# Third part of the weighted one-hot tiles: half of the groups from ScalarE to one VectorE operation, and the gathered dots placed anew

## The chip, the cores and the metric

The kernel runs on one core of a Trainium2 chip. The metric is the device time of one execution in microseconds. TensorE (PE) does matmuls, VectorE (DVE), ScalarE (ACT) and GpSimd (POOL) the rest; SyncE (SP), ScalarE and GpSimd issue DMAs.

## The reference, cut to what matters

A decoder block for 512 tokens of 1024 features: RMSNorm with adaLN, two mixers side by side (windowed attention and gated linear attention), then a retrieval layer over 16384 experts, all in float32. The change is in the last one:

```python
best_v, best_pos = lax.top_k(cand, PEER_TOPK)         # 16 experts for each of 8 heads and token
expert = jnp.take_along_axis(cand_i, best_pos, axis=-1)   # expert = 128 * i1 + i2
gates = jax.nn.softmax(best_v, axis=-1)
...
ub = jnp.take(u, eb, axis=0)                          # 128 experts of each token
hid = jax.nn.gelu(jnp.einsum('tkd,td->tk', ub, xb), approximate=False) * gb
vb = jnp.take(v, eb, axis=0)
return jnp.einsum('tk,tkd->td', hid, vb)
```

## The kernel before

**Tiling.** The tokens are four blocks of 128. Blocks 0, 1 and 2 (DENSE) are done densely: hidden values of all 16384 experts by matmuls, weighted with a gate matrix that is zero for experts a token does not use, then a matmul with v. Block 3 (GB) is done by gathering its rows of u and v (`gu`, `gv`). The last 64 tokens of block 2 (SB) are mixed: their hidden values come from gathered rows of u, while their v side is dense. So the dense u side has 320 tokens (TU).

**The u side.** `u_part(c)` does 128 experts: SP loads `u` (two parts to 1 MB), ScalarE writes the rounded half `his` (L71), VectorE the rest `los` (L72), TensorE does 24 matmuls of 128x320 (L78 to L80) into `ph`, ScalarE the gelu into `ge` (L967), and its queue writes pairs to DRAM (`gsp`, L984).

**The gate matrix.** For each token, `gate_group` makes the 128x128 matrix of its gates as a product of two one-hot matrices, one with a row for the first key and one, weighted by the gate, for the second. Each step, a unit here, takes 8 tokens (TB); a q is 16 tokens, two units (t0 = 0 and 8), and 48 units make the three blocks. A gate in float32 is split into three bf16 parts so that bf16 matmuls add up to it. A unit is

- `one_hot`: one VectorE operation of 128x2048 that writes `o12`, both one-hot tiles, written one unit ahead (L1185);
- `o2`: one VectorE operation that weights the second one-hot tile with parts one and two (`gp3`) (L1204);
- `o3`: eight ScalarE activations of 128x128 that weight it with part three, the float32 remainder `gr3` read as a per-partition scale (L1208);
- 24 matmuls of 128x128 into `pg`, three to a token (L1215), and two ScalarE evictions into `gs` (L1217).

Every second q `gs` is written to `Gd` in DRAM. The parts come from `gate_turn` (L1163, L1164), `gate_parts` (L1170, L1171) and `gate_rest` (L1177).

**The gathered dots.** There are 64 rows of 128 experts. `sp_gather(m)` has POOL issue an indirect DMA of 128 rows of u, 512 KB, into `spr` (L1290), a ring of three; `sp_dot(m)` multiplies and sums on VectorE (L1296) and then issues the gather of row m + 3 into the freed place.

**Order.** VectorE and POOL run in the order in which the code is written; for ScalarE, TensorE and SP a scheduler sets the order. The code is written by generators: `work` chains the head (routing of the blocks, with dots between pieces in `between`, each piece followed by `breath()`, a tiny VectorE operation) and `woven`, once for each block, which takes the four yields of a q (two for each unit) and puts a dot behind each but the first, so three a q. Each piece yields its nominal cost on VectorE and TensorE, and the loop at the end issues a `u_part` whenever TensorE's share lags:

```python
for dd, pp in work:
    d, p = d + dd, p + pp
    while u_ahead.n < NL_U and p * DVE_ALL < (d + LEAD_U) * PE_ALL:
        ...
        d, p = d + 1.14, p + UCOST
```

After this stage the remaining u parts and all v matmuls follow, into six accumulators.

Of the kernel before, what the change touches and what calls it, by code (L numbers as in the profile page):

```python
# [17 lines left out]
P = 128  # L18
D = 1024
# [30 lines left out]
def peer_block_kernel(ctx: ExitStack, tc: tile.TileContext, a: dict, out: bass.AP):  # L50
    nc = tc.nc
# [140 lines left out]
    for L in LW:  # L192
        m = 64 >> L
# [947 lines left out]
    trs = {}  # L1141


    TB = 8

    pair = lambda v: v.rearrange("p (g r) -> p g r", r=2)

    def gate_transposes(n, t1=P):

        t12 = rt.tile([P, P // 2, 2, 2], BF, tag="t12", bufs=2, name=f"t12{n}")  # L1150
        for s in range(2):
            pt = bank(f"tr{s}{n}", BK[s])
            tr = nc.tensor.transpose(pt[:, :P], I12[n][:, s], ident)
            nc.scalar.activation(t12[:, :, s], pair(pt[:, :P]), AF.Copy)
        gp3 = rt.tile([P, P // 2, 2, 2], BF, tag="gp3", bufs=2, name=f"gp3{n}")
        r = rt.tile([P, P], F32, tag="gr3", bufs=2, name=f"gr3{n}")
        trs[n] = [t12, gp3, r, None]
        gate_transposes.tr = gate_transposes.tr or tr
        yield from gate_turn(n, 0, t1)

    def gate_turn(n, t0, t1):
        pt = bank(f"trg{n}{t0}", BK[2])
        nc.tensor.transpose(pt[:, t0:t1], gates[n][t0:t1], ident[t0:t1, t0:t1])  # L1163
        nc.scalar.activation(trs[n][1][:, t0 // 2:t1 // 2, 0], pair(pt[:, t0:t1]), AF.Copy)  # L1164
        trs[n][3] = pt
        yield 0, 0.5

    def gate_parts(n, t0=0, t1=P):
        gp3, r, pt = (pair(t[:, t0:t1]) if len(t.shape) == 2 else t[:, t0 // 2:t1 // 2] for t in trs[n][1:])
        nc.vector.tensor_tensor(r, pt, gp3[:, :, 0], OP.subtract)  # L1170
        nc.scalar.activation(gp3[:, :, 1], r, AF.Copy)  # L1171
        trs[n][3] = None
        yield 0.25, 0

    def gate_rest(n, t0=0, t1=P):
        gp3, r = trs[n][1][:, t0 // 2:t1 // 2], pair(trs[n][2][:, t0:t1])
        nc.vector.tensor_tensor(r, r, gp3[:, :, 1], OP.subtract)  # L1177
# [11 lines left out]
        return o12  # L1189

    def gate_group(bi, n, q):
        gp3, low = trs[n][1:3]
        H = TB // 2
        if q % 2 == 0:
            gate_group.gs = rt.tile([P, P // CG, 2, CG, TG], F32, tag="gs", bufs=2, name=f"gs{n}{q}")
        gs = gate_group.gs
        for t0 in range(0, TG, TB):
            g0 = (q * TG + t0) // 2
            o12 = gate_group.next or one_hot(n, g0)
            gate_group.next = one_hot(n, g0 + H) if g0 + H < P // 2 else None  # L1200
            yield 1.14, 0
            o2 = rt.tile([P, H, 2, P, 2], BF, tag="o2", bufs=3, name=f"o2_{n}{q}{t0}")
            o3 = rt.tile([P, TB, P], BF, tag="o3", bufs=3, name=f"o3_{n}{q}{t0}")
            nc.vector.tensor_tensor(o2, o12[:, :, 1, None].to_broadcast([P, H, 2, P, 2]),  # L1204
                                    gp3[:, g0:g0 + H, :, None].to_broadcast([P, H, 2, P, 2]), OP.mult)
            for i in range(TB):
                g, r = divmod(i, 2)
                nc.scalar.activation(o3[:, i], o12[:, g, 1, :, r], AF.Copy,  # L1208
                                     scale=low[:, 2 * g0 + i:2 * g0 + i + 1])
            for f in range(TB // 4):  # L1210
                pt = bank(f"pg{n}{q}{t0}{f}", BK[f]).rearrange("p (a b) -> p a b", a=4)
                for i in range(4):
                    g, r = divmod(4 * f + i, 2)
                    for m in range(3):
                        nc.tensor.matmul(pt[:, i, :], o12[:, g, 0, :, r], o2[:, g, m, :, r] if m < 2 else o3[:, 4 * f + i],  # L1215
                                         start=(m == 0), stop=(m == 2))
                evict = nc.scalar.activation(gs[:, :, q % 2, :, t0 + 4 * f:t0 + 4 * f + 4],  # L1217
                                             pt.rearrange("p a (c i) -> p c i a", c=P // CG), AF.Copy)
            evicts.append(evict)
            yield 1.14, 1.4  # L1220
        k = bi * (P // TG) + q
        if bi == len(DENSE) - 1:
            nc.scalar.activation(gates_r[0][:, k], gs[:, 0, q % 2], AF.Copy)
        if q % 2:
            writes.append(lambda: (nc.gpsimd if k >= NGRP - 3 else nc.sync).dma_start(
                Gd[:, :, k - 1:k + 1].rearrange("c p g e -> p c (g e)"), gs.rearrange("p c g i t -> p c (g i t)")))
            if k != NGRP - 3:
                writes.pop()()
# [32 lines left out]
    def sp_index(i):  # L1261
        c0, n = SETS[i]
        s0 = c0 - (TD - P)
        if i == 0:
            sp["e"] = rt.tile([P, P], I32, name="spe")
            nc.vector.scalar_tensor_tensor(sp["e"], I12[SB][:, 0], 128.0, I12[SB][:, 1], op0=OP.mult, op1=OP.add)
        sp["ix", i] = rt.tile([P, n], I32, name=f"spix{i}")
        sp["g", i] = rt.tile([P, n], F32, name=f"spg{i}")
        sp["hid", i] = rt.tile([P, n], F32, name=f"sphid{i}")
        for src, key, dt in ((sp["e"], "ix", I32), (gates[SB], "g", F32)):  # L1270
            if i == 0:
                for r in range(P // n):
                    nc.sync.dma_start(sp[key, i][r * n:(r + 1) * n], src[s0:s0 + n, r * n:(r + 1) * n])
            else:
                d = dr.tile([P // n, n, n], dt, name=f"d{key}{i}")
                nc.sync.dma_start(d.rearrange("r t j -> t r j"), src[s0:s0 + n].rearrange("t (r j) -> t r j", j=n))
                nc.sync.dma_start(sp[key, i], d.rearrange("r t j -> (r t) j"))
        if i == 0:
            for j in range(3):
                sp_gather(j)  # L1280
        yield 0.3, 0

# [2 lines left out]
    def sp_gather(m):  # L1285
        i, j = sp_all[m]
        if m == 0:
            sp["r"] = gk.tile([P, 3, D], F32, tag="gring", bufs=1, name="spr")
        sp[m] = sp["r"][:, m % 3]
        nc.gpsimd.indirect_dma_start(out=sp[m], out_offset=None, in_=a["u"],  # L1290
                                     in_offset=bass.IndirectOffsetOnAxis(ap=sp["ix", i][:, j:j + 1], axis=0))

    def sp_dot(m):
        i, j = sp_all[m]
        r = sp.pop(m)
        nc.vector.scalar_tensor_tensor(r, r, 1.0, sp["x", i], op0=OP.mult, op1=OP.mult,  # L1296
                                       accum_out=sp["hid", i][:, j:j + 1])
        if m + 3 < TS:
            sp_gather(m + 3)
        elif m == TS - 1:  # L1300
            sp.pop("r")
        yield 1.15, 0

    def sp_finish(i):
        c0, n = SETS[i]
# [159 lines left out]
    def woven(n, rows, extra, rests={}):  # L1465
        for q in range(P // TG):
            for i, piece in enumerate(gate_group(DENSE.index(n), n, q)):
                yield piece
                if i == 0 and q in rests:
                    yield from rests[q]  # L1470
                if i and rows:
                    yield from sp_dot(rows.pop(0))
                if n == SB and i % 2 and q >= places[0][1]:
                    breath()
                    yield 0.15, 0
            if q in extra:
                yield from chain(*extra[q])
            if writes:
                writes.pop()()

    def breath():
        nc.vector.scalar_tensor_tensor(junk[:, :2], ident[:, :2], 1.0, ident[:, :2], op0=OP.mult, op1=OP.mult,
# [14 lines left out]
    second_block = {1: [route(GB)], 2: [gathered_index()], 6: [gate_transposes(SB, P // 2)], 7: [gate_parts(SB, 0, P // 2)]}
    second_block[7].append(first_place())
# [381 lines left out]
```

## Time and profile before

| | us |
|---|---|
| runs of the kernel before | 1467.71, 1467.70, 1465.24; median 1467.7 |
| profiled execution | 1466.82 |
| its span, first to last instruction | 1465.0, granted clock 0.995 |
| head of the change's stage: routing to the first one-hot tile | 446.1 to 504.9 |
| first two blocks of gates | 504.9 to 702.9 |
| third block of gates | 702.9 to 767.4 |
| its last matmuls | to 776.6 |

A row of a group of instructions names line, engine, operation and tiles, then busy time and mean length in ns, then the idle time before them and what ended it. A row of waits names who waited for whom: microseconds in total, times, and the longest. A timeline row gives start and length in us, and in brackets the idle time before it. A row of windows gives the stretch, its length, the busy time of each engine with the count of its instructions, the granted clock, the busy share of the DMA engines and GB/s.

### The profile page before, as it was taken

Reading aid. Unit: us, or ns where it says so; the run is one execution under the profiler, and the core shown is the slowest. Engines: PE = TensorE matmul, PEld = TensorE weight load, DVE = VectorE, ACT = ScalarE, POOL = GpSimd, SP = SyncE. Lnnn points to the kernel's source line nnn. Section 1 sums busy time; section 2 is a strip of 40 time slices with the busy share of each in tenths; the row PEclk is TensorE's granted clock in tenths of the full one; section 3 lists DMA queues with packets and bytes.
Section 4 is the critical chain, followed back from the end, with each engine's and each line's share of the span. In section 5 each row is a group of like instructions: output and inputs, shape, how many; then the busy total and the mean of one; then the engine's idle time right before and its main releaser. Section 6 shows DMA issues by size and latency. Waiting matters only on the chain. (4 is left out here: it accounts for less than half of the span.)

```text
span 1465.0 us, 23919 instructions
## 1 busy us (share of the span) xinstructions
PE 1408.5 (96%) x9020; PEld 1250.4 (85%) x9020; DVE 1261.0 (86%) x2308; ACT 716.0 (49%) x1299; POOL 603.1 (41%) x401
## 2 busy tenths in 40 slices
PE   5999899999999899999989999999999999999997
PEld 4788788888899899999978888888888888888885
DVE  7777867589999798999976899999999999889996
ACT  4556476533344498878895333233333333232333
POOL 2000000044523344424024676776677676555520
PEclk9999999999999999999999999999999999999999
DMA  9622636354257899999779999999999999999962
GB/s 358 235 87 84 206 113 204 123 189 155 99 195 279 280 319 348 361 347 364 288 254 396 412 412 410 413 412 413 409 410 398 405 372 412 400 411 411 411 252 72
DMA packets 129972, 443.82 MB, mean 303 GB/s; under 512 B 11953, under 2 KB 48577, under 8 KB 109505
## 3 DMA queue, kind: packets, MB, share of 16 engines
q1 hardware_dynamic: 71120, 256.39, 46.3%
q0 software_dynamic: 47136, 171.99, 30.5%
q10 hardware_dynamic: 11600, 13.93, 2.7%
q8 instruction: 70, 1.15, 0.3%
q14 instruction: 46, 0.37, 0.1%
HBM read 399.70 MB, written 42.47 MB: 302 GB/s over the span
## 5 line engine op out<-in xcount | busy, mean ns | idle before, releaser
L78 PE MATMUL ph<-h2Th,his 128*128 128x320 f32 x1024 | 321.5, 314 | 11.0 <-ACT ge L967 9.0
L80 PE MATMUL ph<-h2Th,los 128*128 128x320 f32 x1024 | 317.0, 311 | 2.0 <-DVE los L1654 1.8
L79 PE MATMUL ph<-h2Tl,his 128*128 128x320 f32 x1024 | 316.9, 310 | 0.0
L1342 POOL DMA_INDIRECT gu<-in_u_dram,ix_u x128 | 212.2, 1657 | 149.3 <-DVE gu L1352 80.2
L1377 POOL DMA_INDIRECT gv<-in_vP_dram,ix_v x128 | 206.5, 1613 | 115.5 <-DVE gacc L1382 90.1
L78 PEld LDWEIGHTS ph<-h2Th,his 128*128 128x128 f32 x1024 | 193.6, 189 | 14.1 <-ACT ge L967 11.0
L80 PEld LDWEIGHTS ph<-h2Th,los 128*128 128x128 f32 x1024 | 193.3, 189 | 2.8 <-DVE los L1654 2.0
L79 PEld LDWEIGHTS ph<-h2Tl,his 128*128 128x128 f32 x1024 | 193.8, 189 | 0.8
L1290 POOL DMA_INDIRECT spr<-in_u_dram,spix x64 | 104.9, 1640 | 186.2 <-DVE spr L1296 141.6
L1382 DVE SCALAR_TENSOR_TENSOR gacc<-gv,hg,gacc 128x1024 f32<-128x1024 f32 x127 | 162.6, 1280 | 7.9 <-DMA gv<-in_vP_dram,ix_v 7.6
L78 PE MATMUL acc<-his,Ah 128*128 128x512 f32 x432 | 168.0, 389 | 0.0
L79 PE MATMUL acc<-los,Ah 128*128 128x512 f32 x432 | 168.0, 389 | 0.0
L80 PE MATMUL acc<-his,Al 128*128 128x512 f32 x432 | 168.0, 389 | 0.0
L1352 DVE SCALAR_TENSOR_TENSOR gu<-gu,h2n 128x1024 f32<-128x1024 f32 x128 | 155.7, 1220 | 6.7 <-DMA gu<-in_u_dram,ix_u 6.7
L78 PE MATMUL acc<-hi,Ah 128*128 128x512 f32 x336 | 131.3, 391 | 0.0
L80 PE MATMUL acc<-hi,Al 128*128 128x512 f32 x336 | 131.1, 390 | 0.0
L79 PE MATMUL acc<-lo,Ah 128*128 128x512 f32 x336 | 130.7, 389 | 0.0
L1650 ACT ACTIVATE Ah<-gr 128x768 fp32r<-128x768 f32 x64 | 53.6, 838 | 151.7 <-PE acc L79 128.5
L1208 ACT ACTIVATE o<-o,gr 128x128 bf16<-128x128 bf16 x384 | 121.6, 416 | 7.8 <-DVE o L1185 7.8
L71 ACT ACTIVATE his<-u 128x1024 fp32r<-128x1024 f32 x86 | 90.8, 1057 | 23.4 <-PE ph L79 9.5
L72 DVE TENSOR_TENSOR los<-u,his 128x1024 fp32r<-128x1024 f32 x75 | 91.2, 1218 | 9.7 <-ACT his L71 9.7
L1296 DVE SCALAR_TENSOR_TENSOR spr<-spr,xs 128x1024 f32<-128x1024 f32 x64 | 77.9, 1219 | 23.7 <-DMA spr<-in_u_dram,spix 23.7
(617 smaller groups left out, 2988.0 us busy)
## 6 DMA issues: line engine op xcount, KB each, us to landing
u<-in_uT_dram SPq DMA_DIRECT2D x43, 1024.0 KB
gr<-Gd SPq DMA_DIRECT2D x15, 1536.0 KB
Gd<-gs SPq DMA_DIRECT2D x10, 2048.0 KB
gsp<-ge ACTq DMA_DIRECT2D x40, 320.0 KB
wa<-in_w_ada_dram SPq DMA_DIRECT2D x12, 1024.0 KB
wo<-in_w_out_dram SPq DMA_DIRECT2D x8, 1024.0 KB
wq<-in_wq_dram SPq DMA_DIRECT2D x8, 1024.0 KB
wi<-in_w_in_dram SPq DMA_DIRECT2D x7, 1024.0 KB
```

The costliest lines, as they stand in the source:

```text
L71: nc.scalar.activation(hi, src, AF.Copy)
L72: lo_eng.tensor_tensor(lo, src, hi, OP.subtract)
L78: nc.tensor.matmul(acc, lh, rh, start=start, stop=False)
L79: nc.tensor.matmul(acc, lh, rl, start=False, stop=False)
L80: return nc.tensor.matmul(acc, ll, rh, start=False, stop=stop)
L1208: nc.scalar.activation(o3[:, i], o12[:, g, 1, :, r], AF.Copy, scale=low[:, 2 * g0 + i:2 * g0 + i + 1])
L1290: nc.gpsimd.indirect_dma_start(out=sp[m], out_offset=None, in_=a["u"], in_offset=bass.IndirectOffsetOnAxis(ap=sp["ix", i][:, j:j + 1], axi ...
L1296: nc.vector.scalar_tensor_tensor(r, r, 1.0, sp["x", i], op0=OP.mult, op1=OP.mult, accum_out=sp["hid", i][:, j:j + 1])
L1342: nc.gpsimd.indirect_dma_start(out=ur, out_offset=None, in_=a["u"], in_offset=bass.IndirectOffsetOnAxis(ap=ix_u[:, s:s + 1], axis=0))
L1352: nc.vector.scalar_tensor_tensor(ur, ur, 1.0, h2n, op0=OP.mult, op1=OP.mult, accum_out=hid[:, s:s + 1])
L1377: nc.gpsimd.indirect_dma_start(out=vr, out_offset=None, in_=a["vP"], in_offset=bass.IndirectOffsetOnAxis(ap=ix_v[:, s:s + 1], axis=0))
L1382: nc.vector.scalar_tensor_tensor(gacc, vr, hg[:, s:s + 1], gacc, op0=OP.mult, op1=OP.add)
```

## The change

- For the second unit of each q (t0 = 8, 24 of 48) the third part is made by one VectorE operation of 128x1024 bf16 out of a bf16 copy of the remainder, `gp1`. `gate_rest` writes `gp1` with one more ScalarE activation. For the first unit the eight activations stay.
- `o2` and `o3` become one tile `o2` of three parts, with the same bytes.
- The ring of rows is seven deep until dot 20 (HEAD): three places as before and four in a tile `spr2`, which borrows a buffer of `gs`; it is three deep from then on.
- The head holds 20 dots in place of 13, and two more breaths. The other 44 are spread singly, 44 over 51 places, by a counter in `woven`.
- The planner's nominal VectorE sum has 5.16 for each q in place of 4.56, and a unit with t0 = 8 yields 1.74 in place of 1.14.

```diff
+        gp1 = rt.tile([P, P // 2, 2], BF, tag="gp1", bufs=2, name=f"gp1{n}")
...
     def gate_rest(n, t0=0, t1=P):
...
         nc.vector.tensor_tensor(r, r, gp3[:, :, 1], OP.subtract)
+        nc.scalar.activation(trs[n][3][:, t0 // 2:t1 // 2], r, AF.Copy)
...
-            o2 = rt.tile([P, H, 2, P, 2], BF, tag="o2", bufs=3, name=f"o2_{n}{q}{t0}")
-            o3 = rt.tile([P, TB, P], BF, tag="o3", bufs=3, name=f"o3_{n}{q}{t0}")
+            o2 = rt.tile([P, H, 3, P, 2], BF, tag="o2", bufs=3, name=f"o2_{n}{q}{t0}")
...
-            for i in range(TB):
-                g, r = divmod(i, 2)
-                nc.scalar.activation(o3[:, i], o12[:, g, 1, :, r], AF.Copy,
-                                     scale=low[:, 2 * g0 + i:2 * g0 + i + 1])
+            if t0:
+                nc.vector.tensor_tensor(o2[:, :, 2], o12[:, :, 1], gp1[:, g0:g0 + H, None].to_broadcast([P, H, P, 2]),
+                                        OP.mult)
+            else:
+                for i in range(TB):
+                    g, r = divmod(i, 2)
+                    nc.scalar.activation(o2[:, g, 2, :, r], o12[:, g, 1, :, r], AF.Copy,
+                                         scale=low[:, 2 * g0 + i:2 * g0 + i + 1])
...
-            yield 1.14, 1.4
+            yield (1.74 if t0 else 1.14), 1.4
...
-            for j in range(3):
+            for j in range(7):
                 sp_gather(j)
...
-        sp[m] = sp["r"][:, m % 3]
+            sp["r2"] = rt.tile([P, 4, D], F32, tag="gs", bufs=2, name="spr2")
+        k = m % 7 if m < HEAD else m % 3
+        sp[m] = sp["r"][:, k] if k < 3 else sp["r2"][:, k - 3]
...
-        if m + 3 < TS:
-            sp_gather(m + 3)
-        elif m == TS - 1:
+        while sp_dot.next < min(TS, m + 8 if sp_dot.next < HEAD else m + 4):
+            sp_gather(sp_dot.next)
+            sp_dot.next += 1
+        if m == TS - 1:
...
                 if i and rows:
-                    yield from sp_dot(rows.pop(0))
+                    woven.place += 1
+                    if TS - len(rows) < HEAD + woven.place * (TS - HEAD) / 51:
+                        yield from sp_dot(rows.pop(0))
...
-    head = (route(SB), sp_index(0), sp_rows(0), between(route(0), (0, 0, 0)), gate_transposes(0), between(route(1), (3, 3, 3)),
-            between(gate_parts(0), (2,)), between(gate_rest(0), (2,)))
+    head = (route(SB), sp_index(0), sp_rows(0), between(route(0), (0, 0, 1)), gate_transposes(0), between(route(1), (3, 3, 3)),
+            between(gate_parts(0), (3,)), between(gate_rest(0), (3,)), between(iter([(0, 0)] * 2), (2, 2)))
...
-    DVE_ALL = 11 + 4 * 7.6 + 3 + 1.15 * TS + 2.28 * 2 * NGRP + 1.15 * EARLY + 1.14 * (NL_U - WQ_U)
+    DVE_ALL = 11 + 4 * 7.6 + 3 + 1.15 * TS + 5.16 * NGRP + 1.15 * EARLY + 1.14 * (NL_U - WQ_U)
```

What moves, at three places. VectorE at the first units, in the kernel before (the number after `o12_` is block and token pair, after `o2_` block, q and t0; `los<-u84` is the rest half of a u part):

```order
L1296 SCALAR_TENSOR_TENSOR spr_4610,sphid0_4605<-spr_4610,xs0_4645 128x1024
L1185 TENSOR_TENSOR o12_00_5129<-iot_3212,t120_4767 128x2048
L1185 TENSOR_TENSOR o12_04_5131<-iot_3212,t120_4767 128x2048
L72 TENSOR_TENSOR los_2207<-u80_5095,his_2206 128x1024
L1204 TENSOR_TENSOR o2_000_5162<-o12_00_5129,gp30_4774 128x2048
L1296 SCALAR_TENSOR_TENSOR spr_4610,sphid0_4605<-spr_4610,xs0_4645 128x1024
L1185 TENSOR_TENSOR o12_08_5203<-iot_3212,t120_4767 128x2048
L72 TENSOR_TENSOR los_2207<-u84_5205,his_2206 128x1024
L1296 SCALAR_TENSOR_TENSOR spr_4610,sphid0_4605<-spr_4610,xs0_4645 128x1024
L1204 TENSOR_TENSOR o2_008_5238<-o12_04_5131,gp30_4774 128x2048
```

The same place of VectorE in the change:

```order
L1305 SCALAR_TENSOR_TENSOR spr2_4611,sphid0_4605<-spr2_4611,xs0_4621 128x1024
L1187 TENSOR_TENSOR o12_00_5208<-iot_3212,t120_4774 128x2048
L1187 TENSOR_TENSOR o12_04_5210<-iot_3212,t120_4774 128x2048
L72 TENSOR_TENSOR los_2207<-u84_5174,his_2206 128x1024
L1205 TENSOR_TENSOR o2_000_5241<-o12_00_5208,gp30_4781 128x4x512
L1305 SCALAR_TENSOR_TENSOR spr_4610,sphid0_4605<-spr_4610,xs0_4621 128x1024
L1187 TENSOR_TENSOR o12_08_5281<-iot_3212,t120_4774 128x2048
L72 TENSOR_TENSOR los_2207<-u85_5283,his_2206 128x1024
L1305 SCALAR_TENSOR_TENSOR spr_4610,sphid0_4605<-spr_4610,xs0_4621 128x1024
L1205 TENSOR_TENSOR o2_008_5316<-o12_04_5210,gp30_4781 128x4x512
L1208 TENSOR_TENSOR o2_008_5316<-o12_04_5210,gp10_4782 128x4x256
```

The row order is the same, with the new operation at the end of every second unit; the u parts are two further on (u84 for u80), which stand ahead of the first one-hot tile now.

ScalarE at the first units, in the kernel before:

```order
L967 ACTIVATE ge72_4959<-ph74_4991 128x320
L71 ACTIVATE his_2206<-u80_5095 128x1024
L984 DMA gsp_2208<-ge72_4959 128x2x320
L967 ACTIVATE ge76_5024<-ph76_5027 128x320
L71 ACTIVATE his_2206<-u84_5205 128x1024
L1208 ACTIVATE o3_000_5163<-o12_00_5129,gr30_4775 128x128 x8
L967 ACTIVATE ge76_5024<-ph78_5062 128x320
L71 ACTIVATE his_2206<-u84_5205 128x1024
L1208 ACTIVATE o3_008_5239<-o12_04_5131,gr30_4775 128x128 x8
```

ScalarE there in the change:

```order
L967 ACTIVATE ge76_5039<-ph78_5074 128x320
L71 ACTIVATE his_2206<-u84_5174 128x1024
L1165 ACTIVATE gp31_5803<-trg10_5806 128x64x2
L984 DMA gsp_2208<-ge76_5039 128x2x320
L967 ACTIVATE ge80_5108<-ph80_5111 128x320
L967 ACTIVATE ge80_5108<-ph82_5142 128x320
L984 DMA gsp_2208<-ge80_5108 128x2x320
L71 ACTIVATE his_2206<-u85_5283 128x1024 x2
L1213 ACTIVATE o2_000_5241<-o12_00_5208,gr30_4783 128x128 x8
L967 ACTIVATE ge84_5176<-ph84_5179 128x320
```

Before, the second gelu of ge76 stands behind the first eight activations of the third part; in the change two gelus more (ge80) and both halves of u85 stand ahead of them.

ScalarE near the end of the third block, in the kernel before:

```order
L1217 ACTIVATE gs24_8339<-pg2400_8382 128x16x8x4
L1208 ACTIVATE o3_248_8413<-o12_236_8340,gr32_7682 128x128
L1208 ACTIVATE o3_250_8455<-o12_240_8410,gr32_7682 128x128 x2
L1217 ACTIVATE gs24_8339<-pg2401_8396 128x16x8x4
L1208 ACTIVATE o3_250_8455<-o12_240_8410,gr32_7682 128x128 x4
L1217 ACTIVATE gs24_8339<-pg2480_8423 128x16x8x4
L1223 ACTIVATE gr0_7835<-gs22_8135 128x128
L1208 ACTIVATE o3_250_8455<-o12_240_8410,gr32_7682 128x128 x2
L1208 ACTIVATE o3_258_8528<-o12_244_8452,gr32_7682 128x128 x8
```

The same place in the change:

```order
L71 ACTIVATE his_2206<-u8_8571 128x1024
L1213 ACTIVATE o2_250_8275<-o12_240_8211,gr32_7557 128x128 x7
L1222 ACTIVATE gs24_8168<-pg2400_8183 128x16x8x4
L1213 ACTIVATE o2_250_8275<-o12_240_8211,gr32_7557 128x128
L1222 ACTIVATE gs24_8168<-pg2401_8197 128x16x8x4
L967 ACTIVATE ge0_8135<-ph2_8215 128x320
L71 ACTIVATE his_2206<-u8_8571 128x1024
L1222 ACTIVATE gs24_8168<-pg2480_8244 128x16x8x4
L1222 ACTIVATE gs24_8168<-pg2481_8258 128x16x8x4
```

The evictions of a unit with t0 = 8 (pg2480, pg2481) now follow one another with no third-part activations between; those of o3_248 and o3_258 are gone.

More of the change, by code (lines that the diff above doesn't have):

```diff
@@ L1155, in gate_transposes @@
         gp3 = rt.tile([P, P // 2, 2, 2], BF, tag="gp3", bufs=2, name=f"gp3{n}")
+        gp1 = rt.tile([P, P // 2, 2], BF, tag="gp1", bufs=2, name=f"gp1{n}")
         r = rt.tile([P, P], F32, tag="gr3", bufs=2, name=f"gr3{n}")
-        trs[n] = [t12, gp3, r, None]
+        trs[n] = [t12, gp3, r, gp1, None]
         gate_transposes.tr = gate_transposes.tr or tr
@@ L1164, in gate_turn @@
         nc.scalar.activation(trs[n][1][:, t0 // 2:t1 // 2, 0], pair(pt[:, t0:t1]), AF.Copy)
-        trs[n][3] = pt
+        trs[n][4] = pt
         yield 0, 0.5
     def gate_parts(n, t0=0, t1=P):
-        gp3, r, pt = (pair(t[:, t0:t1]) if len(t.shape) == 2 else t[:, t0 // 2:t1 // 2] for t in trs[n][1:])
+        gp3, r, pt = trs[n][1][:, t0 // 2:t1 // 2], pair(trs[n][2][:, t0:t1]), pair(trs[n][4][:, t0:t1])
         nc.vector.tensor_tensor(r, pt, gp3[:, :, 0], OP.subtract)
         nc.scalar.activation(gp3[:, :, 1], r, AF.Copy)
-        trs[n][3] = None
+        trs[n][4] = None
         yield 0.25, 0
@@ L1191, in gate_group @@
     def gate_group(bi, n, q):
-        gp3, low = trs[n][1:3]
+        gp3, low, gp1 = trs[n][1:4]
         H = TB // 2
@@ L1201, in gate_group @@
             yield 1.14, 0
-            o2 = rt.tile([P, H, 2, P, 2], BF, tag="o2", bufs=3, name=f"o2_{n}{q}{t0}")
-            o3 = rt.tile([P, TB, P], BF, tag="o3", bufs=3, name=f"o3_{n}{q}{t0}")
-            nc.vector.tensor_tensor(o2, o12[:, :, 1, None].to_broadcast([P, H, 2, P, 2]),
+            o2 = rt.tile([P, H, 3, P, 2], BF, tag="o2", bufs=3, name=f"o2_{n}{q}{t0}")
+            nc.vector.tensor_tensor(o2[:, :, :2], o12[:, :, 1, None].to_broadcast([P, H, 2, P, 2]),
                                     gp3[:, g0:g0 + H, :, None].to_broadcast([P, H, 2, P, 2]), OP.mult)
-            for i in range(TB):
-                g, r = divmod(i, 2)
-                nc.scalar.activation(o3[:, i], o12[:, g, 1, :, r], AF.Copy,
-                                     scale=low[:, 2 * g0 + i:2 * g0 + i + 1])
+            if t0:
[6 more added lines that the diff above has]
+                                         scale=low[:, 2 * g0 + i:2 * g0 + i + 1])
             for f in range(TB // 4):
@@ L1214, in gate_group @@
                     for m in range(3):
-                        nc.tensor.matmul(pt[:, i, :], o12[:, g, 0, :, r], o2[:, g, m, :, r] if m < 2 else o3[:, 4 * f + i],
+                        nc.tensor.matmul(pt[:, i, :], o12[:, g, 0, :, r], o2[:, g, m, :, r],
                                          start=(m == 0), stop=(m == 2))
@@ L1288, in sp_gather @@
             sp["r"] = gk.tile([P, 3, D], F32, tag="gring", bufs=1, name="spr")
-        sp[m] = sp["r"][:, m % 3]
+            sp["r2"] = rt.tile([P, 4, D], F32, tag="gs", bufs=2, name="spr2")
+        k = m % 7 if m < HEAD else m % 3
+        sp[m] = sp["r"][:, k] if k < 3 else sp["r2"][:, k - 3]
+        if m == HEAD:
+            sp.pop("r2")
         nc.gpsimd.indirect_dma_start(out=sp[m], out_offset=None, in_=a["u"],
@@ L1297, in sp_dot @@
                                        accum_out=sp["hid", i][:, j:j + 1])
-        if m + 3 < TS:
-            sp_gather(m + 3)
-        elif m == TS - 1:
+        while sp_dot.next < min(TS, m + 8 if sp_dot.next < HEAD else m + 4):
+            sp_gather(sp_dot.next)
+            sp_dot.next += 1
+        if m == TS - 1:
             sp.pop("r")
         yield 1.15, 0
+    HEAD = 20
+    sp_dot.next = 7
     def sp_finish(i):
@@ L1479, in woven @@
                 writes.pop()()
+    woven.place = 0
     def breath():
```

## The prediction

> **What bounds the kernel now.** The profiled execution took 1466.8 us, 0.9 below the median of 1467.7; its span is 1465.0 us, and the sum below goes against its own times. First the busy times on the page, then the stretches around the change: routing and the head up to the first one-hot tile at 504.9 us, the first two blocks of gate building to 702.9, the third block to 767.4, its last matmuls to 776.6, and the rest.
>
> ```profile
> PE 1408.5 (96%) x9020; PEld 1250.4 (85%) x9020; DVE 1261.0 (86%) x2308; ACT 716.0 (49%) x1299; POOL 603.1 (41%) x401
> ```
>
> ```profile
> core 0: us, PE busy (x) PEld busy (x) DVE busy (x) ACT busy (x) POOL busy (x), PEclk, DMA share, GB/s
> 446.10:504.90 58.80, 58.05 (x399) 57.77 (x398) 47.96 (x84) 22.57 (x36) 23.06 (x15) 1.00 0.87 310
> 504.90:702.90 198.00, 188.75 (x1702) 184.21 (x1703) 184.92 (x226) 162.69 (x407) 80.06 (x48) 0.98 0.95 343
> 702.90:767.40 64.50, 58.83 (x602) 55.01 (x600) 52.77 (x68) 61.20 (x177) 8.75 (x6) 1.00 0.74 253
> 767.40:776.60 9.20, 9.11 (x82) 8.54 (x80) 2.31 (x4) 6.29 (x18) 2.96 (x3) 1.00 1.01 346
> 777.00:1465.00 688.00, 674.76 (x3328) 583.38 (x3328) 616.14 (x661) 240.31 (x238) 410.93 (x251) 0.99 0.95 381
> ```
>
> TensorE bounds the whole. Behind 777 it is busy 674.8 of 688 us, so an earlier end of the stage carries through to the end of the program. Inside the stage it idles 0.75 + 9.25 + 5.67 + 0.09 = 15.8 us, and VectorE has hardly more room: 10.8, 13.1 and 11.7 us idle in the first three stretches. The two pace each other here; ScalarE joins them in the third block with 61.2 of 64.5 us. What ended the idle times, in the head, in the first two blocks and in the third:
>
> ```profile
> DVE spr L1296 <- DMA spr<-in_u_dram,spix: 10.8, 4, 4.8
> ```
>
> ```profile
> DVE spr L1296 <- DMA spr<-in_u_dram,spix: 17.7, 13, 4.8
> PE ph L78 <- ACT ge L967: 8.2, 5, 4.9
> ACT o L1208 <- DVE o L1185: 7.8, 1, 7.8
> ACT his L71 <- DMA u<-in_uT_dram: 6.1, 4, 3.2
> ```
>
> ```profile
> DVE o L1185 <- PE pg L1215: 5.2, 3, 4.1
> PE pg L1215 <- ACT gs L1217: 3.2, 5, 1.8
> DVE gr L1170 <- ACT gp L1164: 3.0, 1, 3.0
> DVE gr L1177 <- ACT gp L1171: 2.6, 1, 2.6
> ```
>
> (The 4.8 us wait lies across the cut and counts in the first two answers; the 17.7 are 12.9 without it.) So VectorE waits for gathered rows, and in the third block for ScalarE and for a TensorE that waits for ScalarE. The timeline shows how the worst one reaches TensorE:
>
> ```profile
> 503.80 1.23 DVE L1296 SCALAR_TENSOR_TENSOR spr<-spr,xs 128x1024 f32<-128x1024 f32 x1 [4.80 <-DMA spr<-in_u_dram,spix]
> 504.95 2.36 DVE L1185 TENSOR_TENSOR o<-iot,t 128x2048 bf16<-128x2048 bf16 x2
> 507.23 1.22 DVE L72 TENSOR_TENSOR los<-u,his 128x1024 fp32r<-128x1024 f32 x1
> 508.36 1.22 DVE L1204 TENSOR_TENSOR o<-o,gp 128x2048 bf16<-128x2048 bf16 x1
> 506.21 2.44 ACT L1208 ACTIVATE o<-o,gr 128x128 bf16<-128x128 bf16 x8 [7.78 <-DVE o L1185]
> 503.59 0.31 PE L79 MATMUL ph<-h2Tl,his 128*128 128x320 f32 x1
> 503.73 0.31 PE L80 MATMUL ph<-h2Th,los 128*128 128x320 f32 x1
> 503.88 0.27 PE L1163 MATMUL trg<-ident,g 128*128 128x128 f32 x1
> 509.03 0.64 PE L78 MATMUL ph<-h2Th,his 128*128 128x320 f32 x1 [4.87 <-ACT ge L967]
> 509.46 0.47 PE L79 MATMUL ph<-h2Tl,his 128*128 128x320 f32 x1
> 509.73 0.47 PE L80 MATMUL ph<-h2Th,los 128*128 128x320 f32 x1
> ```
>
> A dot stood 4.8 us for its row; the first one-hot tiles stood behind it on VectorE; ScalarE's first eight third-part activations stood before the gelu that frees the next PSUM bank (o3_000 ahead of ge76 in the order shown above); TensorE stopped for 4.87 us. It then ran at a spacing of 0.27 us (509.46 to 509.73) until about 514.3, where it had 0.14 to 0.15 before (503.59, 503.73, 503.88). Twenty matmuls at 0.12 us extra are another 2.4.
>
> **The change part by part.** The prices first, and two rows on the gathers:
>
> ```profile
> L1208 ACT ACTIVATE o<-o,gr 128x128 bf16<-128x128 bf16 x384 | 121.6, 416 | 7.8 <-DVE o L1185 7.8
> L1117 DVE TENSOR_TENSOR oh<-oh 128x1024 bf16<-128x1024 bf16 x8 | 5.2, 688 | 0.0
> L1482 DVE SCALAR_TENSOR_TENSOR junk<-ident 128x2 f32<-128x2 f32 x14 | 2.1, 153 | 0.0
> ```
>
> ```profile
> L1290 POOL DMA_INDIRECT spr<-in_u_dram,spix x11: 1678/1680/1684, 505.3 to 543.4; - x11
> 498.98 0.94 POOL L1290 DMA_INDIRECT spr<-in_u_dram,spix  x1 [0.30 <-issue]
> ```
>
> *The new VectorE operation.* 24 of them, 1024 bf16 each. Their line is not in this trace. The lower bound is L1117, of the same size and types: 0.69 us, or 0.61 start to start, since two operations on VectorE overlap by 0.08 (504.95 to 507.23 are two of 1.22 in 2.28). The upper bound is the 128x1024 operation at the price of one without the bf16 rate, 1.13 start to start (L72, 507.23 to 508.36). I take 0.61: the operation at L1204, with the same broadcast operands, takes the 1.22 of L1185, so 1.14 start to start for 2048 elements, of which half is 0.57 and a start of its own. 24 x 0.61 = 14.6 us more on VectorE, 1 part in 20 of the stage. The Trainium skill ("VectorE: DVE Perf Modes", section "Mode 2×_1P") asks for 16-bit operands with step one on every side, and the new operation meets it, its broadcast pair of weights included; by that rule the sum is the one below, and without it 24 x 0.52 = 12.5 us longer.
>
> *The activations that go.* Eight at 0.29 us start to start (eight take 2.44 at 506.21), 2.35 us a unit, 24 units: 56 us off ScalarE, 18.8 of them in the third block, where the 61.2 busy us become about 43. Four activations of some 0.3 us come in for gp1; their results are read only a unit later, from the second unit on.
>
> *Dots and ring.* Seven dots move into the head (20 for 13): 7 x 1.15 = 8.0 us of VectorE there, six of them out of the two blocks and one out of the third. The head also gets two more u parts (los halves, 2 x 1.14 = 2.3; TensorE gets their 48 matmuls there as well) and two breath() pairs, 2 x 0.23 = 0.5. Seven rows are in flight in place of three, so that a row has the time of seven dots to come round, 8.0 us of VectorE's at the least, where it had three. The gathers on POOL are issued as before by the dot that frees the row, so behind every dot one instruction of 0.94 to 1.68 us on POOL; POOL is busy 23 of 58.8 us. DMA carries in the head 310 GB/s x 58.8 us = 18.2 MB, and now 7 x 0.52 + 2 x 0.52 = 4.7 MB more in about 62 us: 370 GB/s, below the 381 that the last stretch averages. It is close, so I keep 3 us of the 10.8 us of waits (bounds 0 and 10.8).
>
> *The middle.* VectorE: 184.9 + 16 x 0.61 - 6 x 1.15 - 2.3 = 185.5 us. Its dots fill 44 of 51 places: with about 49 of them before, three took 184.9/49 x 3 = 11.3 us, now 185.5/43 x 3 = 12.9. The ring of three gains 1.6 us a turn, and the 12 waits left had a mean of 12.9/12 = 1.1. I keep 4.5 of the 12.9 (bounds 0 and 12.9).
>
> *The third block.* VectorE: 52.8 + 8 x 0.61 - 1.15 = 56.5. Of its 11.7 us of idle time 5.2 are a wait for TensorE, which itself waited for gs evictions among the third-part activations, and 5.6 are waits for ScalarE's gp parts. Both have ScalarE's full queue for a cause:
>
> ```profile
> 709.00:773.60 64.60, 58.84 (x607) 54.68 (x606) 48.98 (x61) 64.11 (x188) 7.70 (x5) 1.00 0.76 257
> 752.03 3.12 ACT L1208 ACTIVATE o<-o,gr 128x128 bf16<-128x128 bf16 x10
> 755.91 0.68 ACT L1217 ACTIVATE gs<-pg 128x512 f32<-128x512 f32 x1
> 754.31 1.23 DVE L1185 TENSOR_TENSOR o<-iot,t 128x2048 bf16<-128x2048 bf16 x1 [4.05 <-PE pg L1215]
> ```
>
> ScalarE has 0.5 us free in 64.6; ten third-part operations stand in a row ahead of an eviction. With half of them gone I keep 2.5 us of idle (bounds 0 and 11.7). The last matmuls behind VectorE's end stay 9.2 us.
>
> *Sum.* Head 58.8 (47.96 + 8.0 + 2.3 + 0.5), middle 185.5, third 56.5, end 9.2: 310.0 us without a wait, so TensorE's stage would end at 446.1 + 310.0 = 756.1. With 3 + 4.5 + 2.5 = 10 us of waits it is 766.1 against 776.6: 10.5 us earlier. TensorE must be able to: of 330.5 us it idled 15.8 and lost 2.4 to the clock, so 18 is the most, and 10.5 leaves it 7.7. The forecast is 1466.8 - 10.5 = 1456.3, put at 1456. Break-even stands at 776.6 - 756.1 = 20.5 us of waits, against 35.4 before (10.8 + 12.9 + 11.7).
>
> **Rivals.** *Slower: the dots' waits stay.* Place: the dots in the head and the middle. If DMA cannot bring rows sooner (0.95 busy in the middle) the 23.7 us of waits stay and VectorE, with 14.6 us more of its own, is the bound: 756.1 + 23.7 + 2.5 = 782.3, 5.7 later, 1472.5; it decides above 20.5 us of waits in all. For it: DMA's share; against: the middle moves six gathers and two u parts less (4.2 of 68 MB). The Trainium skill ("SBUF — State Buffer", section "Who interferes with whom") has a rule on that side: a VectorE instruction with two inputs in SBUF contends with a GpSimd instruction that reads SBUF, and the one that issues first holds the lock. The trace has both lengths of a gather, 0.94 and 1.68 us; by that rule the new operations could hold up the gathers by 24 x 0.61/44 = 0.33 us each, an estimate from the rows above, and 12 waits would grow by 4 us, to 1460.
>
> *No change: only head and third block gain.* The middle keeps its 12.9 us: 766.1 + 8.4 = 774.5, 1464.7.
>
> *No change: the new operation runs at the slow price.* 766.1 + 12.5 = 778.6, 1468.8.
>
> *Faster still.* Waits near 3 us, TensorE loses almost nothing: 759, 1449; TensorE's 18 us allow 1449 at the best. For it speaks that the largest stall is one of 4.87 + 2.4 us with a single cause that is gone.
>
> **How the numbers follow.** No change means within 0.2%, 2.9 us. The forecast has 0.62 (own range 1452 to 1461), faster still 0.16, the two of no change 0.08 and 0.04, slower 0.10. Faster is 0.62 + 0.16 = 0.78, same 0.12, slower 0.10. The range from 1449 to 1466 leaves out the slow price, the slower case and little at the fast end: 0.2 at most.
>
> **What would show it.** The new line near 0.69 us mean, 24 times; ScalarE some 43 us busy in the third block; VectorE's waits for gathered rows down from 23.7 to some 7.5 us; no stop of TensorE over 3 us at the first one-hot tile and its clock full there; the stage's last gate matmul some 10 us earlier and the rest as long as before. It is wrong if these waits stay above 18 us, if the new line takes 1.2, or if a new wait in the third block (VectorE for TensorE, or a u half for its load) comes in at 5 us or more.

## The result, and the profile after

The changed kernel took 1453.7 us (median of 6 runs, 1451.7 to 1459.4) against 1467.7 (1465.2 to 1469.1): 0.991 of the time, 95% interval 0.989 to 0.993. Once more, beside the last experiments on another chip, it took 1452.1 against 1469.8, 0.9885 (0.9856 to 0.9914). The profiled execution took 1454.6 us, with a span of 1452.8.

The windows of the changed kernel, cut at the same places as before: start of the stage (the indices of the gathered rows are made, 446.10 before), first one-hot tile, third block, end of VectorE's part, last matmul of the stage, end. Columns as in the prediction.

```profile
0.00:449.76 449.76, 422.61 (x2904) 364.93 (x2905) 356.17 (x1272) 222.29 (x425) 77.39 (x79) 0.98 0.48 169
449.76:509.23 59.47, 59.47 (x411) 59.45 (x410) 58.35 (x106) 24.31 (x41) 35.92 (x23) 1.00 0.94 373
509.23:697.88 188.65, 188.14 (x1729) 184.07 (x1729) 184.68 (x228) 126.81 (x279) 69.01 (x41) 1.00 0.94 340
697.88:753.70 55.82, 53.77 (x565) 51.39 (x563) 54.31 (x70) 46.99 (x124) 10.03 (x5) 1.00 0.84 286
753.70:763.10 9.40, 9.37 (x91) 9.16 (x92) 4.07 (x6) 3.12 (x6) 4.07 (x4) 1.00 0.99 365
763.10:1452.80 689.70, 676.22 (x3331) 584.55 (x3329) 616.24 (x661) 239.99 (x238) 417.47 (x249) 0.99 0.95 380
```

The stage takes 313.3 us (449.76 to 763.10), 17.0 less than the 330.3 before (446.10 to 776.40, cut at the same matmul). TensorE's idle time in it falls from 15.8 to 0 + 0.5 + 2.05 + 0.03 = 2.6 us. The start of the stage lies 3.7 us later in this execution, at a granted clock of 0.98 where it was 1.00; the delay is there by 230 us, where the two programs are the same, and in the other profile of the changed kernel the stage starts at 444.3. Behind the stage it is 1.1 us more. 17.0 - 3.7 - 1.1 = 12.2, the difference of the spans.

VectorE's and TensorE's waits of the changed kernel, in the first two blocks and then in the third:

```profile
DVE spr L1305 <- DMA spr<-in_u_dram,spix: 3.8, 5, 1.2
PE ph L78 <- ACT ge L967: 0.5, 2, 0.3
```

```profile
DVE o L1187 <- PE pg L1220: 1.5, 1, 1.5
PE pg L1220 <- DVE o L1205: 1.3, 1, 1.3
```

The dots (now L1305) wait 4.1 us for rows with the 0.3 of the head, where it was 23.7. TensorE stands 0.5 us for gelus where it was 8.2, and the chain of gate parts behind ScalarE (3.0 and 2.6) is gone. The groups of the new line and of the eight activations that stay, in the stage:

```profile
L1208 DVE TENSOR_TENSOR o<-o,gp 128x1024 bf16<-128x1024 bf16 x24 | 16.4, 685 | 0.0
L1213 ACT ACTIVATE o<-o,gr 128x128 bf16<-128x128 bf16 x192 | 60.7, 436 | 0.0
```

### The profile page after: what moved, and what is told of

It is laid out like the page before. It is cut to its first block, busy times and chain, and to the rows that moved or that the text cites. A ratio compares the mean times of both kernels' runs of the same rounds, so it can differ in the third digit from the quotient of the medians.

```text
span 1452.8 us, 23754 instructions
## 1 busy us (share of the span) xinstructions
PE 1409.6 (97%) x9020; PEld 1253.6 (86%) x9020; DVE 1273.8 (88%) x2336; ACT 663.5 (46%) x1111; POOL 613.9 (42%) x401
## 4 chain that ended last, share of the span: by engine, by line
PE 75%; DVE 9%; issue 6%; DMA 4%; ACT 3%; POOL 3%; SPq 0%; ACTq 0%; POOLq 0%; DVEq 0%
PE acc L78 12%; PE acc L80 12%; PE acc L79 12%; PE ph L80 8%; PE ph L78 8%; PE ph L79 8%; POOL spr L1299 3%; DMA wa<-in_w_ada_dram 2%; PE pg L1220 2%; PE pj L474 1%; DVE macc L240 1%; PE pj L78 1%; DVE los L72 1%; PE pj L79 1%; PE pj L80 1%
## 5 line engine op out<-in xcount | busy, mean ns | idle before, releaser
L1355 POOL DMA_INDIRECT gu<-in_u_dram,ix_u x128 | 216.1, 1688 | 145.8 <-DVE gu L1365 81.0
L1390 POOL DMA_INDIRECT gv<-in_vP_dram,ix_v x128 | 213.1, 1665 | 110.3 <-DVE gacc L1395 86.7
L1299 POOL DMA_INDIRECT spr<-in_u_dram,spix x64 | 104.9, 1639 | 170.8 <-DVE spr L1305 128.7
L79 PEld LDWEIGHTS acc<-los,Ah 128*128 128x128 f32 x432 | 81.1, 188 | 16.9
L80 PEld LDWEIGHTS acc<-his,Al 128*128 128x128 f32 x432 | 81.1, 188 | 16.8
```

Source lines behind the costliest of these rows:

```text
L79: nc.tensor.matmul(acc, lh, rl, start=False, stop=False)
L80: return nc.tensor.matmul(acc, ll, rh, start=False, stop=stop)
L1355: nc.gpsimd.indirect_dma_start(out=ur, out_offset=None, in_=a["u"], in_offset=bass.IndirectOffsetOnAxis(ap=ix_u[:, s:s + 1], axis=0))
L1390: nc.gpsimd.indirect_dma_start(out=vr, out_offset=None, in_=a["vP"], in_offset=bass.IndirectOffsetOnAxis(ap=ix_v[:, s:s + 1], axis=0))
```

## The experiments

Each kernel ran next to the kernel before, four kernels to a chip. "Idle" is TensorE's idle time in the head, in the first two blocks and in the third up to the stage's last matmul, from the windows of the kernel's own profile; the third block begins with its first one-hot tile. "rows" is what the dots wait for rows in the whole stage. Times are medians; the profiled execution, to which the last three columns belong, can lie some us off (dots alone 4.9 above its median, third part alone and ring alone 2.8 below, third block only with old dots 6.9 below).

| kernel | us | before | ratio (95%) | stage | idle | rows |
|---|---|---|---|---|---|---|
| before | 1467.7 | | | 330.3 | 0.8, 9.2, 5.8 | 23.7 |
| the change | 1453.7 | 1467.7 | 0.991 (0.989 to 0.993) | 313.3 | 0, 0.5, 2.1 | 4.1 |
| dots alone | 1459.7 | 1468.7 | 0.9936 (0.9913 to 0.9959) | 325.3 | 0, 4.7, 7.4 | 7.8 |
| third part alone | 1461.0 | 1468.7 | 0.994 (0.9917 to 0.9964) | 323.5 | 1.9, 5.6, 1.3 | 16.0 |
| all units | 1459.1 | 1468.7 | 0.9929 (0.9908 to 0.995) | 323.2 | 0.8, 2.6, 3.1 | 0.6 |
| operation twice | 1467.0 | 1468.7 | 0.9992 (0.9974 to 1.0009) | 328.9 | 0, 7.5, 5.3 | 3.3 |
| third block only | 1449.9 | 1468.0 | 0.9877 (0.9857 to 0.9896) | 310.0 | 0, 1.9, 0 | 11.7 |
| old planner | 1459.1 | 1468.0 | 0.994 (0.9916 to 0.9964) | 318.2 | 0, 3.7, 3.6 | 9.6 |
| ring of three | 1468.3 | 1468.0 | 1.0002 (0.9985 to 1.0018) | 333.8 | 6.2, 6.0, 2.1 | 24.3 |
| 13 in the head | 1453.8 | 1468.0 | 0.9897 (0.9878 to 0.9916) | 316.2 | 0, 2.6, 1.3 | 8.8 |
| third block only, 13 in the head | 1458.6 | 1469.8 | 0.9935 (0.9912 to 0.9958) | 321.0 | 0, 4.2, 4.9 | 16.4 |
| ring alone | 1460.9 | 1469.8 | 0.9949 (0.9931 to 0.9966) | 321.8 | 0, 3.6, 5.5 | 15.1 |
| third block only, old dots | 1469.1 | 1469.8 | 1.0 (0.9978 to 1.0023) | 323.3 | 0.6, 5.2, 4.3 | 20.6 |
| the change again | 1452.1 | 1469.8 | 0.9885 (0.9856 to 0.9914) | 315.3 | 0, 1.3, 2.3 | 7.1 |

My theory was that the dots' waits cost the head and the first two blocks, and ScalarE's full queue the third. The rivals: all of it is ScalarE's relief, or all of it the dots.

### The dots alone

```diff
-            if t0:
+            if False:
...
-            yield (1.74 if t0 else 1.14), 1.4
+            yield (1.74 if False else 1.14), 1.4
...
-    DVE_ALL = ... 5.16 * NGRP ...
+    DVE_ALL = ... 4.56 * NGRP ...
```

> The new ring and the new places of the dots alone; all 48 third parts stay on ScalarE, and the planner has the sums of the kernel before. Theory (the dots' waits cost the head and the first two blocks, ScalarE's full queue the third): waits for gathered rows fall from 23.7 to about 5 us, the 4.87 us stop of TensorE at the first one-hot tile is gone, the first 252 us of the stage shorten by 9 to 12 us, the third block with its end stays within 3 us of its 73.5; time 1455 to 1459. Rival (all of the gain is ScalarE's relief): 1464 to 1468. Rival (the dots are all of the gain): 1452 to 1455, the third block short too.

Measured: 1459.7, a little above the range. TensorE's stop at the first one-hot tile is gone, and the third block, 76.2 us long, idles TensorE for 7.4, as the theory says. The first two stretches shorten by 7.7 us, less than the 9 to 12 expected, and the dots still wait 7.8 us for rows where I expected 5. The waits in the third block:

```profile
DVE gr L1178 <- ACT gp L1172: 10.6, 2, 7.6
PE pg L1220 <- ACT gs L1222: 4.5, 4, 2.0
```

VectorE stands 10.6 us for a gate part that sits behind third-part activations on ScalarE, TensorE 4.5 us for evictions. Neither rival gives both halves, and the time fits neither.

### The third part alone

```diff
-            for j in range(7):
+            for j in range(3):
                 sp_gather(j)
...
-        sp[m] = sp["r"][:, k] if k < 3 else sp["r2"][:, k - 3]
...
+        sp[m] = sp["r"][:, m % 3]
...
-    HEAD = 20
+    HEAD = 13
...
-    head = (... the dots 1, 3 3 3, 3, 3, 2 2 ...)
+    head = (... the dots 0, 3 3 3, 2, 2 ...)
```

> The VectorE third part for half of the units alone; ring of three, 13 dots in the head, three dots to a q as before. Theory: the third block gains some 8 us, the first two blocks lose some 3 to 8 because VectorE has 9.8 us more there with its waits for rows (23.7 before, I expect 12 to 24) still in; time 1461 to 1469. Rival (all of the gain is ScalarE's relief): 1452 to 1456. Rival (the dots are all of the gain): 1470 or more, with the third block at its 73.5 us or longer.

Measured: 1461.0, at the fast end of the theory's range. The third block takes 66.4 us for 73.5, near the 8 us expected, and TensorE's idle time there falls to 1.3 us. The head and the first two blocks together take 257.1 us for 256.8; in the latter I had expected a loss, and idle time fell from 9.2 to 5.6. The dots' wait there:

```profile
DVE spr L1301 <- DMA spr<-in_u_dram,spix: 7.5, 6, 4.0
```

It was 12.9 with the same ring and the same dots. The 16 new operations stand between dots, and a row has that much longer to come; that this is the reason is argued, since ScalarE is relieved there too. Apart the two parts are worth 9.1 and 7.7 us, 16.8 as a sum, and together 14.0 to 17.7: the medians do not show that one takes from the other.

### All units, and the operation twice

```diff
-            if t0:
+            if True:
...
-            yield (1.74 if t0 else 1.14), 1.4
+            yield (1.74 if True else 1.14), 1.4
...
-    DVE_ALL = ... 5.16 * NGRP ...
+    DVE_ALL = ... 5.76 * NGRP ...
```

> The changed kernel with the VectorE third part for all 48 units, the planner's sums to match. Theory (VectorE is now as full as TensorE: 58.4 of 59.5, 184.7 of 188.7, 54.3 of 55.8 us busy): 24 more operations of 0.61 are 14.6 us, of which 4 to 6 fall into idle time; 8 to 11 us slower than the change, 1461 to 1465. Rival (TensorE alone bounds it, VectorE has room): within 3 us of the change. Rival (ScalarE still costs): faster than the change, 1450 or less.

```diff
+                for _ in range(2):
                     nc.vector.tensor_tensor(o2[:, :, 2], o12[:, :, 1], gp1[...]..., OP.mult)
```

> The changed kernel with the new VectorE operation done twice into the same tile; nothing else moves, ScalarE's work as in the change. Theory: as for the kernel with all units on VectorE, 8 to 11 us slower than the change, since only VectorE's 14.6 us count; equal to it within 3 us. If ScalarE's relief still counts, this one is slower than that one by more than 3 us. Rival (VectorE has room): within 3 us of the change.

Measured: 1459.1 and 1467.0, where both were expected at 1461 to 1465; they gain 9.6 and 1.7 us where the change gains 14.0 to 17.7. VectorE has no room for 24 operations more. That the two would be equal was wrong. ScalarE's waits for its u halves in the first two blocks, all units first, the operation twice second:

```profile
ACT his L71 <- DMA u<-in_uT_dram: 7.3, 4, 2.4
```

```profile
ACT his L71 <- DMA u<-in_uT_dram: 20.5, 6, 5.1
```

The second differs in the relief of ScalarE and in the planner, which does not know of the second operation. Which of the two makes the later loads is open.

### The third block only

```diff
-            if t0:
+            if n == SB and t0:
...
-            yield (1.74 if t0 else 1.14), 1.4
+            yield (1.74 if n == SB and t0 else 1.14), 1.4
...
-    DVE_ALL = ... 5.16 * NGRP ...
+    DVE_ALL = ... 4.56 * NGRP + 4.8 ...
```

> The changed kernel with the VectorE third part only in the third block (8 units); the 16 units of the first two blocks have ScalarE's activations again. Theory (ScalarE's full queue costs in the third block alone): the third block's lost time of TensorE falls as in the change (6.3 to about 1.3 us), and the time is 4 to 6 us below that of the dots alone, 1453 to 1456. Rival (the operations in the first two blocks help as well, by relief of ScalarE there or because VectorE's longer work lets the rows arrive): within 3 us of the dots alone, 1456 to 1460.

Measured: 1449.9, below every range, and the fastest kernel here. Its windows (first two blocks, third block) and the dots' wait in the former:

```profile
510.60:694.20 183.60, 181.69 (x1677) 178.10 (x1677) 173.14 (x211) 159.06 (x404) 69.07 (x41) 1.00 0.95 339
694.20:747.70 53.50, 53.50 (x564) 52.15 (x563) 53.00 (x67) 46.45 (x121) 6.74 (x5) 1.00 0.87 300
```

```profile
DVE spr L1305 <- DMA spr<-in_u_dram,spix: 11.4, 8, 3.0
```

Of the 11.4 us one wait of 1.2 belongs to the last dot of the head. The dots wait 10.2 us in the first two blocks, longer than in the change (3.8, and 5.9 in its second profile), and TensorE idles 1.9 us of 183.6. VectorE is busy 173.1 us there for the change's 184.7; the waits fall into the room that this leaves and cost nothing that shows. Against the change the intervals touch (0.9877 with 0.9857 to 0.9896, and 0.991 with 0.989 to 0.993 or 0.9885 with 0.9856 to 0.9914), and they were not run on one chip: that the 16 other operations cost some 4 us with these dots is likely and not shown; a gain from them does not show.

### The old planner

```diff
-            yield (1.74 if t0 else 1.14), 1.4
+            yield 1.14, 1.4
...
-    DVE_ALL = ... 5.16 * NGRP ...
+    DVE_ALL = ... 4.56 * NGRP ...
```

> The changed kernel with the planner's numbers of the kernel before (4.56 for each q, 1.14 for each unit). Theory (these numbers move a u part by one or two places and nothing else): within 2 us of the change, 1452 to 1456. Rival (the u parts' new places carry a part of the gain): 3 us or more slower than the change, 1457 and above.

Measured: 1459.1, on the rival's side. Its interval (0.9916 to 0.9964) meets that of the change in its first set of runs and lies just above that of the second (0.9856 to 0.9914). ScalarE and TensorE in its timeline:

```profile
624.62 1.06 ACT L71 ACTIVATE his<-u 128x1024 fp32r<-128x1024 f32 x1 [3.27 <-DMA u<-in_uT_dram]
625.59 2.47 ACT L1213 ACTIVATE o<-o,gr 128x128 bf16<-128x128 bf16 x8
628.39 0.47 PE L78 MATMUL ph<-h2Th,his 128*128 128x320 f32 x1 [3.44 <-ACT ge L967]
```

A u half came late; eight third-part activations stood behind it, and the gelu that frees TensorE's bank behind these. That the u parts' places decide whether such a chain meets is argued from this one place.

This kernel and the dots alone differ in the new operation alone, and gain the same, 8.9 and 9.1 us. So with the planner's old sums the operation brings no time that shows, though TensorE's idle time in the third block falls from 7.4 to 3.6 us. What the operation is worth hangs on where the u parts stand; the new sums without the operation were not run, and their own part of the gain stays open.

### The ring of three

```diff
-            for j in range(7):
+            for j in range(3):
                 sp_gather(j)
...
-        sp[m] = sp["r"][:, k] if k < 3 else sp["r2"][:, k - 3]
...
+        sp[m] = sp["r"][:, m % 3]
...
```

> The changed kernel with the ring of three rows throughout; still 20 dots in the head. Theory (the depth of the ring is what ends the waits): the head waits 14 to 20 us for rows in place of 0.3, part of it regained since fewer dots are left: 4 to 9 us slower than the change, 1458 to 1463. Rival (the places of the dots matter, not the ring): within 3 us of the change.

Measured: 1468.3, the whole gain gone and 5 us more than I expected. Its head:

```profile
DVE spr L1301 <- DMA spr<-in_u_dram,spix: 18.1, 10, 5.3
PE ph L80 <- DVE los L72: 5.8, 3, 3.8
```

The waits are as large as expected; I had not priced that TensorE stands for the u halves queued behind the dots on VectorE, three times, nor the clock: the head's granted clock is 0.93 where the change has 1.00.

### 13 dots in the head

```diff
-    HEAD = 20
+    HEAD = 13
...
-    head = (... the dots 1, 3 3 3, 3, 3, 2 2 ...)
+    head = (... the dots 0, 3 3 3, 2, 2 ...)
```

> The changed kernel with 13 dots in the head (at their old places, without the two more breaths), the ring seven deep for these 13 and three deep after; the other 51 at all 51 places. Theory (the ring counts, and VectorE's longer work hides the rows in the first two blocks, as the kernel with the third part alone showed with 3.5 us of waits there): 0 to 4 us slower than the change, 1453 to 1458. Rival (the dots must leave the first two blocks): 5 us or more slower, 1459 and above, with 10 us or more of waits for rows there.

Measured: 1453.8, the change's time. The 3.5 us of waits that the theory names were counted to a point 14 us ahead of the third block; up to its first one-hot tile they are 7.5. Here they are 8.8, for 3.8 in the change. TensorE idles 2.6 us there for 0.5. With the ring of seven and the new operations in all blocks, moving seven dots buys no time that shows.

### Ring alone, third block with either, and the change again

The ring alone is the dots alone with the edit of the last experiment: VectorE's order is that of the kernel before (gp1 and the joint o2 tile stay in).

> The kernel before with the ring of seven for its 13 dots in the head and nothing else: dots at their old places, all third parts on ScalarE, the planner's old numbers. Theory (the ring's depth is all of the dots' part): 1457 to 1460, as with all of the new dots. Rival (the 20 dots in the head are needed for that part): 1462 to 1467, with 8 us or more of waits for rows left in the first two blocks.

Measured: 1460.9, 0.9 us above the theory's range and 1.1 below the rival's, with the rival's sign of 8 us or more of waits: neither is right as it stands. Head, first two blocks, and third block to its end, then the dots' wait in the first two blocks:

```profile
444.90:492.90 48.00, 48.00 (x332) 47.99 (x332) 47.97 (x84) 20.45 (x35) 24.92 (x16) 1.00 0.94 359
492.90:692.90 200.00, 196.37 (x1771) 191.93 (x1771) 184.65 (x226) 164.97 (x411) 78.40 (x47) 1.00 0.95 343
692.90:766.70 73.80, 68.34 (x681) 63.71 (x680) 55.13 (x69) 67.78 (x195) 9.45 (x8) 1.00 0.78 265
```

```profile
DVE spr L1305 <- DMA spr<-in_u_dram,spix: 15.1, 10, 4.2
```

VectorE's head takes its busy time, 48.0 us for 58.8, and TensorE no longer stops for 4.87 us. That is 8.9 us with the waits of the first two blocks all still there, and the third block as slow as ever (73.8 for 73.5).

The third block only with the same 13 dots, and the third block only with ring and dots as before:

> The VectorE third part in the third block only (8 units), the ring of seven for 13 dots in the head at their old places, three dots to a q behind it. Theory (two separate causes: the ring's depth ends the waits, eight operations in the third block free ScalarE there; the 16 other operations cost some 4 us and moving seven dots is worth nothing): as the kernel with the third block only and 20 dots, 1448 to 1452, 2 to 6 us faster than the change. Rival (moving dots out of the first two blocks counts once VectorE's longer work there is gone): 1453 to 1457.

> The kernel before with eight VectorE third parts in the third block and nothing else new (ring of three, 13 dots in the head, the planner's sums with 4.8 us more). Theory (separate causes): 1460 to 1464, that is 4 to 7 us for the third block. Rival (the third block's gain shows only with the waits for rows gone): 1465 to 1469. Rival (the third part alone was worth 8 us because of this block and of nothing else): 1458 to 1461.

Measured: 1458.6 and 1469.1; the theory of separate causes fails at both, and the times lie at the rivals' side, 1.6 and 0.1 us above their ranges. The first, VectorE then TensorE, at the start of the third block:

```profile
695.56 1.23 DVE L1305 SCALAR_TENSOR_TENSOR spr<-spr,xs 128x1024 f32<-128x1024 f32 x1 [3.85 <-DMA spr<-in_u_dram,spix]
696.71 0.22 DVE L1171 TENSOR_TENSOR gr<-trg,gp 128x64 f32<-128x64 f32 x1
696.85 2.35 DVE L1187 TENSOR_TENSOR o<-iot,t 128x2048 bf16<-128x2048 bf16 x2
699.12 1.22 DVE L72 TENSOR_TENSOR los<-u,his 128x1024 fp32r<-128x1024 f32 x1
700.39 0.63 PE L80 MATMUL ph<-h2Th,los 128*128 128x320 f32 x1 [3.86 <-DVE los L72]
```

A dot waits 3.85 us where two one-hot operations follow in a row (each block begins so) and a u half stands behind them: TensorE stops for 3.86. The second kernel has the same stop at that place, 2.98 us behind a wait of 3.34. In the kernel before the stop at the first block began in the same way, with a late row ahead of two one-hot operations; from there it reached TensorE through ScalarE's activations, and here through the u half. Here the seven dots do count: with 20 in the head the same kernel is at 0.9877 and has no stop over 1.2 us ahead of the stage's last matmul. (The profile of the second is of the shortest of its runs, 1462.2, and its stage is 7.0 us shorter than before; what the longer runs lose it does not show.)

> The changed kernel once more, on the chip of the other three, to compare with them. Every theory: 1452 to 1456.

Measured: 1452.1, as expected.

## Why the prediction was right, and where it was not

The time, 1453.7, is 2.3 us below the 1456 and inside the forecast's own range of 1452 to 1461; the gain is 14.0 us in the medians (10.5 us were forecast for the profiled execution). Its mechanism held in the stage: the late rows and ScalarE's queue are both in it, and a kernel that leaves out the one or the other keeps 7.7 or 9.1 us of the gain. What it did not price is the planner's new sums: with the old ones both parts together gain 8.9 us, no more than the dots alone.

- *The new operation.* 685 ns, 24 times, as taken; the slow price is out. By the Trainium skill ("VectorE: DVE Perf Modes", section "Mode 2×_1P") 16-bit operands with step one take the fast mode: the trace agrees. Of the rule on the shared port ("SBUF — State Buffer", section "Who interferes with whom"), in the Trainium skill, nothing shows: a gather takes 1639 ns in the mean where it took 1640.
- *The head.* Kept 3 us of waits; 1.1 us of VectorE's time was idle. It grew by 0.6 us for seven more dots. The ring did it (with the ring of three the dots wait 18.1 us there).
- *The middle.* Forecast 190.0 us, measured 188.65; waits 3.8 for the 4.5 kept (5.9 in the second profile). Both things that the forecast took to lengthen the ring's turn go with shorter waits: 7.5 us with the new operations alone and 7.8 with the new dots alone, from 12.9; neither does it by itself.
- *The third block.* Forecast 68.2 us to its last matmul, measured 65.2. This term was mis-sized by 3.0 us: VectorE was idle 1.5 and not 2.5, and busy 54.3 and not 56.5. ScalarE was busy 47.0 us there for the 43 forecast. That its queue held the block up is shown by the dots alone (TensorE idle 7.4) against the old planner (3.6), which differ in the new operation alone; the planner's new sums bring it to 2.1.
- *The sum.* 17.0 us in the stage for the 10.5 forecast, head 2.3, middle 1.3 and third block 3.0 us better than forecast; 3.7 ahead of the stage and 1.1 behind it made up for most of it in this execution. That its 1454.6 came so near the 1456.3 is luck; the second set's 1452.1 lies at the edge of the range. I took 18 us as the most there is and 7.7 as what TensorE would go on losing; it kept 2.6 us of idle time. The rival "faster still" describes the stage better than the forecast does.
- *What the sum could not see.* It adds VectorE's work and its waits, and asks of no wait whether it reaches TensorE. Its break-even of 20.5 us stands where one kernel tried it: with the ring of three VectorE idles 18.1 us in the head and 6.7 in the first two blocks, and the time is 1.0002 of before. But the third block only has 17.8 us of idle time on VectorE in its stage, more than the change's 11.9, and is the fastest, with TensorE idle for 1.9; VectorE has 9.2 us less work in it, and the longer waits fall into that room. What counts is whether a waiting dot, or a late u half, stands just ahead of what TensorE needs next.
- *The slower rival* had DMA unable to bring rows sooner. In the head the DMA share rose from 0.87 to 0.94 (373 GB/s) and the rows came.

## What to carry to other kernels

On an engine that takes its work in order, price a wait by what is queued behind it and who needs that, not by its length: dots waited 10.2 us in one kernel while TensorE idled 1.9, and in another a single wait of 3.85 us stopped it for 3.86. A deeper ring of buffers took such waits out of the head for 8.9 us without moving an instruction on VectorE; with operations put between dots the waits of the blocks behind it fell from 12.9 to 7.5. Relief of an engine that is full pays only where nothing else stops the stage: with the deep ring and the thinned dots eight operations in the third block gave no less than all 24; with 13 dots in the head they gave less (0.9935 of before, for 0.9897), and with the ring of three nothing (1.0, for 0.994). And moving work on one engine moves what a planner places beside it: try the two apart.

## What the runs showed of the chip

TensorE can fall to half speed behind a stop as short as 2 us. With the dots alone, behind a stop of 1.99 us, the matmuls start 0.27 us apart from the second on, at a granted clock of 0.51; with the ring of three, behind one of 2.26 us, they start 0.15 apart at once, at 1.00:

```profile
625.56 0.63 PE L78 MATMUL ph<-h2Th,his 128*128 128x320 f32 x1 [1.99 <-ACT ge L967]
625.99 0.47 PE L79 MATMUL ph<-h2Tl,his 128*128 128x320 f32 x1
626.26 0.47 PE L80 MATMUL ph<-h2Th,los 128*128 128x320 f32 x1
```

```profile
525.82 0.41 PE L80 MATMUL ph<-h2Th,los 128*128 128x320 f32 x1 [2.26 <-DVE los L72]
526.07 0.31 PE L78 MATMUL ph<-h2Th,his 128*128 128x320 f32 x1
526.22 0.31 PE L79 MATMUL ph<-h2Tl,his 128*128 128x320 f32 x1
```

Nor does it always follow at once: behind a stop of 2.37 us the half speed came from the second matmul on with the dots alone (683.47), and from the fourth on in the ring of three (613.50). So the length of a stop alone does not tell whether and when the half speed follows; what else does is not shown here.
